# Two branches of an MLP cross SBUF in one transfer, and the fifth pair of sets is computed earlier

## The chip, the cores and the metric

The kernel runs on one core of a Trainium2 chip. The metric is the device time of one execution in microseconds (us). The kernel is written in Python; a scheduler places its instructions on the engines and sets every semaphore, and each engine then runs its own queue in order. The order of a queue follows the program's order in the main, but the scheduler may bring an instruction forward that it expects to be ready before an earlier one.

## The reference, cut to what matters

The model is an encoder trunk of two layers on 256 tokens of 1024 channels. Each layer has a mixer (pooling, attention, gates) and an MLP. Only the MLP is touched by the change:

```python
def _conv_ffn(xn, w_up, conv_w, conv_b, w_down):
    a, gval = jnp.split(xn @ w_up, 2, axis=-1)
    a = lax.conv_general_dilated(a, conv_w[:, None, :], ..., feature_group_count=D_FF) + conv_b
    return (jax.nn.gelu(a) * gval) @ w_down
```

`w_up` is 1024 x 5632 and `w_down` 2816 x 1024, all float32. The convolution has width 3 along the tokens, one filter per channel. The two halves of `xn @ w_up` are called the branches a and g here. 2816 channels are 22 chunks of 128.

## The kernel before

**Products.** Each float32 matrix is split into a high and a low part, and a product is made of three matmuls: high by high, high by low, low by high. For weights, `Weights` does this piece by piece: SP loads 1 MB of a weight matrix into one of three `raw` buffers (L120), ScalarE rounds half of it to the high part `wh` (L180), VectorE subtracts to get the low part `wl` (L181). So one load gives two pieces. Five pieces may be alive at once, and a piece is asked for three pieces ahead of its use. The next load is issued on SP when the buffer of the load three before is free, that is when the `wl` of both its pieces are done.

**Stages of the MLP.** `ORDER` (L39) writes out the order by hand. An entry `a`n or `g`n is a set: the a or g branch of the chunks 4n to 4n+3, made by `by_rows` (L599) from four pieces, 12 matmuls of 512 columns for each piece. `r5` is the last set: chunks 20 and 21 of both branches together. An entry `d`n is part n of the down projection, for chunks 4n to 4n+3, `residual_mm` (L528), again 12 matmuls for each chunk and one chunk a piece. Chunks 18 to 21 are held back and multiplied at the end, in segments, so that the residual sum and the norm of the next sub-layer can begin early. After each piece the function `unit()` (L1203) is called; so an entry of `ORDER` is four units, and the MLP has 64.

**From rows to channels.** A set comes out of `by_rows` with tokens on partitions, but the convolution and the down projection want channels there. `turn_up` (L1124) has VectorE transpose blocks of 32 x 32 (L1139, one instruction for each half t of the tokens) into a tile called `up_at`, and then `cross` (L611) has SP issue 16 DMAs that move the 32-partition blocks across partitions within SBUF. `cross` is a generator: each `unit()` takes it one step on, which is four DMAs (L616). Every set crosses by itself: a DMA moves 32 partitions x 256 floats, that is 32 KB in runs of 1 KB. The rows of all sets take turns in two buffers in the tile of tag `at2`. The g sets arrive in two buffers in the tile of tag `xn` (`up_xn` in the profile), the a sets and `r5` in tiles of the tags `gates` and `v0` (`up_turned`).

**Chunks.** `CHUNKS` (L40) says after which unit the chunk f is worked on by `up(f)` (L1150): ScalarE copies the crossed a chunk (L1155) and applies the middle tap and bias (L1157), VectorE adds the other taps (L1158, L1161), four more steps make the gelu (L1168, L1169, L1172, L1173), VectorE multiplies by the crossed g chunk (L1177), and L1180 and L1181 split the result in two parts for the down projection.

**Ends of the layers.** In the first layer, four pieces of the next layer's weights are split into the tags `m2`, `ybig` and `at2` while the down projection ends. Then L429 adds the sums to the residual, `Norm` (L417) squares and scales, and TensorE turns the result (L465).

Of the kernel before, what the change touches and what calls it, by code (L numbers as in the profile page):

```python
# [10 lines left out]
F32 = mybir.dt.float32  # L11
# [5 lines left out]
P = 128  # L17
# [10 lines left out]
NF = DFF // P  # L28
# [7 lines left out]

WARM = (5, 1, 2, 1)
PAIRS = (2, 4, 0, 1, 3, 5)
ORDER = "a0 g0 a1 g1 a2 g2 d0 a3 g3 d1 a4 g4 r5 d2 d3 d4"  # L39
CHUNKS = (13, 15, 17, 19, 21, 23, 25, 27, 29, 31, 33, 35, 41, 43, 45, 47, 53, 54, 56, 57, 58, 60)  # L40
VISITS = ((0, 1, 12, 14), (2, 3, 15, 16), (9, 10, 22, 23), (10, 11, 23, 24))
HALVES = (slice(0, 512), slice(512, D))
SEGMENTS = (HALVES, (slice(0, 512), slice(512, 768), slice(768, D)))
# [164 lines left out]
def encoder(ctx, tc, x, w_in, w_pool, pool_scale, w_a, w_b, w_o, norm1, norm2, w_up, conv_w,  # L208
# [4 lines left out]
    big = ctx.enter_context(tc.tile_pool(name="big", bufs=1))  # L213
# [15 lines left out]
    def rows(w, r0, n=2, c0=0, width=1024, tag=None, pieces=2):  # L229

        src = w[r0 : r0 + n * P, c0 : c0 + width].rearrange("(k p) c -> p k c", p=P)
        h = n // pieces
        return W.add(
            src, (n, width), [((lambda t, j=j: t[:, j * h : (j + 1) * h, :]), (h, width)) for j in range(pieces)],
            tag,
        )

    for l in range(DEPTH):
        for g in range(NG):
            c0 = C_V + g * 512  # L240
            slots = (("m2", 0, 2), ("m2", 1, 2), ("ybig",), ("at2",)) if g == 0 else ()
            for j in range(2):
                tag = "k1" if l == 0 and g == 1 and j == 0 else None
# [30 lines left out]
        slots = (("v1",), ("ybig",), ("at2",))  # L274
        for kind, n in ORDER.split():
            n = int(n)
            for j in range(2):
# [14 lines left out]
                else:  # L292
                    p = rows(w_up[l], j * 512, 4, (kind == "g") * DFF + 4 * n * P, 512)
# [7 lines left out]
    def gain(src):  # L301
        g = sm.tile([P, 2 * D], F32, tag="gain", bufs=1, name="gain")[:, 0:D]
        nc.sync.dma_start(out=g, in_=src.partition_broadcast(P))
        return g
# [281 lines left out]
    def v_tile():  # L586
        return acc.tile([P, 512], F32, tag="acc", name="v_ps")

    def v_sum(ps, x2, t, n, piece, of=4):

        _, (wh, wl) = piece
        passes = [(0, wh, 0), (0, wl, 0), (1, wh, 0), (0, wh, 1), (0, wl, 1), (1, wh, 1)]
        for m, (part, w, j) in enumerate(passes):
            nc.tensor.matmul(  # L594
                ps, x2[:, 2 * n + j, part, t, :], w[:, j, :], start=(n + m == 0),
                stop=(n == of - 1 and m == 5),
            )

    def by_rows(x2, of, visit=None):  # L599

        ps = [mmp.tile([P, 512], F32, tag="mm", name="rows_ps") for _ in range(2)]
        for n in range(of):
            piece = W.get()
            for t in range(2):
                v_sum(ps[t], x2, t, n, piece, of)
            W.free(piece[0])
            if visit:
                visit()
        return ps

    def cross(out, in_):  # L611

        for i in range(4):
            for j in range(4):
                a, b = slice(32 * i, 32 * i + 32), slice(32 * j, 32 * j + 32)
                nc.sync.dma_start(out=out[b, i], in_=in_[a, j])  # L616
            yield
# [174 lines left out]
    for l in range(DEPTH):  # L792
# [25 lines left out]
        else:  # L818
            for g in range(NG):
                held = begun[0] if g == 0 else [W.get() for _ in range(4)]  # L820
                for t in range(2):
                    if g + t == 0:
                        ps = begun[1]
                    else:
                        ps = v_tile()
# [15 lines left out]
        for gi in range(3, -1, -1):  # L841
# [8 lines left out]
            cur, n = u, S + 2 * PAD  # L850
            sh = 1
            while sh < w:
# [3 lines left out]
                    out=nxt[:, :, 0:n], in0=cur[:, :, 0:n], in1=cur[:, :, sh : sh + n]  # L856
# [7 lines left out]
            if hw > 1:  # L864
                e = edge[:, gi, hw : w - 1].unsqueeze(1).to_broadcast([P, 2, hw - 1])
                r = slice(o + S - hw + 1, o + S)
# [3 lines left out]
                out=pd, in0=cur[:, :, o : o + S], scalar=1.0 / w, in1=u[:, :, PAD : PAD + S],  # L870
# [34 lines left out]
        at2 = big.tile([P, HPG, 2, 2, P], F32R, tag="at2", name="at2")  # L905
        probs, ptiles, split, crossing = {}, {}, {}, []
# [90 lines left out]
        for m, c in enumerate(PAIRS):  # L997
# [4 lines left out]
            for n in range(4):  # L1002
# [5 lines left out]
                if hd < HPG:  # L1008
# [3 lines left out]
                        out=lo[:, hd], in0=src, scalar=scale, in1=hi[:, hd].bitcast(F32),  # L1012
# [3 lines left out]
                        out=lo[:, hd], in0=rest, scalar=scale, in1=lo[:, hd].bitcast(F32),  # L1016
                        op0=ALU.mult, op1=ALU.add,
                    )
                else:
# [3 lines left out]
                        out=o, in0=src, scalar=scale, in1=o, op0=ALU.mult, op1=ALU.add  # L1023
# [4 lines left out]
        for n, cc in enumerate(HALVES):  # L1028
            ps = by_rows(x2, 4, step)
# [30 lines left out]
        def keep_merged(c0, t, m):  # L1060
# [9 lines left out]
        g2 = gain(norm2[l])  # L1070
        nc.vector.transpose(
            out=way[:, 0].rearrange("p j t c r -> p (t c) j r"),
# [37 lines left out]
        g1 = gain(norm1[l + 1] if l + 1 < DEPTH else norm_f)  # L1110
# [8 lines left out]
        acts = {}  # L1119


        turned, ways = {}, []

        def turn_up(key, ps, tag):  # L1124

            if not ways:
                for own in ("at2", "xn"):
                    t = big.tile([P, 2, 4, 2, 4, 32], F32, tag=own, name="up_" + own)
                    ways.append([t[:, 0], t[:, 1]])
                ways.append([])  # L1130
            rows = ways[0].pop(0)
            ways[0].append(rows)
            if tag is None:
                out = ways[1].pop(0)
                ways[1].append(out)
            else:
                out = big.tile([P, 4, 2, 4, 32], F32, tag=tag, name="up_turned")
            for t in range(2):
                nc.vector.transpose(  # L1139
                    out=rows[:, :, t].rearrange("p j c r -> p c j r"),  # L1140
                    in_=ps[t].rearrange("p (c j r) -> p c j r", c=4, j=4),
                )
            ways[2].append(cross(out, rows))
            turned[key] = out.rearrange("p i t c r -> p c t i r")

        def blocks_in_order(a):

# [53 lines left out]
        count, chunk = 0, 0  # L1201

        def unit():  # L1203
            nonlocal count, chunk
            count += 1
            if ways and ways[2] and next(ways[2][0], "end") == "end":
                ways[2].pop(0)
                if ways[2]:
                    next(ways[2][0])
            while chunk < NF and CHUNKS[chunk] < count:  # L1210
                up(chunk)
                chunk += 1

        for kind, n in ORDER.split():
            if kind == "d":
                for _ in range(4):
                    next(down)
                    unit()
                continue
            if (kind, n) == ("a", "0"):  # L1220
                held, ps = entry
                ps = [ps, v_tile()]
                for k in range(4):
                    v_sum(ps[1], x2, 1, k, held[k])
                    unit()
                for i, _ in held:
                    W.free(i)
            else:
                ps = by_rows(x2, 4, unit)
            n = int(n)  # L1230
            turn_up((kind, n), ps, None if kind == "g" else ("gates", "v0")[n % 2])
        assert chunk == NF
        if l + 1 < DEPTH:
            x2 = two_parts("x", "x2")
            late["norm"] = Norm(to_channels(x2, mmp, g1))
# [33 lines left out]
```

## Time and profile before

| what | value |
|---|---|
| median of 3 runs | 878.66 us |
| lowest and highest of them | 875.95 and 880.52 us |
| the profiled execution | 878.63 us |
| its span, first to last instruction | 876.9 us |
| mean granted TensorE clock | 0.994 |
| VectorE busy | 653.6 us (75%) |
| ScalarE busy | 481.6 us (55%) |

The profiled execution lies 0.03 us from the median, and 1.73 us of it lie outside the span. Times in the rows below are microseconds from the start of the span. PE is TensorE's matmul, PEld its weight load, DVE is VectorE, ACT is ScalarE, SP is the engine whose queue issues the loads and the crossings. L12 is line 12 of the kernel. Where a row of the timeline has a count, several instructions are merged in it. The time in square brackets at the end of a row is the engine's idle time before it, with what ended it.

### The profile page before, as it was taken

To read this page: it belongs to the slowest core of one execution; us is meant where nothing else is said; L and a number is where in the kernel's file an instruction comes from. 1 tells how busy PE (TensorE), PEld (TensorE's weight loads), DVE (VectorE), ACT (ScalarE), POOL (GpSimd) and SP (SyncE) were. 2 spreads that over 40 slices of the span, in tenths; PEclk is the share of its full clock that TensorE was granted. 3 is DMA by queue.
4 is the path that set the end of the run, shared out by engine and by line. 5 is a ranking of instruction groups with operands and counts; after the bars stand their busy time and mean duration, and the time that the engine had idled before them with its cause. 6 is when DMAs were issued, how large, how long until landed. Compare 5 with 4: busy or idle time off the path is not lost.

```text
span 876.9 us, 11882 instructions
## 1 busy us (share of the span) xinstructions
PE 858.1 (98%) x4234; PEld 725.0 (83%) x4234; DVE 653.6 (75%) x1016; ACT 481.6 (55%) x777; POOL 21.2 (2%) x53
## 2 busy tenths in 40 slices
PE   9999999999999999999899999999999999999996
PEld 7888988888888887878788899888888888877885
DVE  6998786756866887688855968775567777876885
ACT  7755554543645656646635555454444456655573
POOL 2020000000000000000000000000000000000001
PEclk9999999999999999999999999999999999999998
DMA  9676546665737667666826455547557266676661
GB/s 333 211 221 222 202 129 211 191 224 185 265 117 232 200 221 255 216 196 211 313 101 219 165 194 191 178 158 243 202 195 272 96 220 197 225 237 213 222 224 48
DMA packets 114623, 178.76 MB, mean 204 GB/s; under 512 B 10542, under 2 KB 61950, under 8 KB 114564
## 3 DMA queue, kind: packets, MB, share of 16 engines
q1 hardware_dynamic: 114052, 176.67, 60.1%
q0 software_dynamic: 496, 1.33, 0.6%
q8 instruction: 33, 0.54, 0.2%
q14 instruction: 26, 0.21, 0.1%
q10 hardware_dynamic: 16, 0.00, 0.0%
HBM read 160.12 MB, written 1.07 MB: 184 GB/s over the span
## 4 chain that ended last, share of the span: by engine, by line
PE 85%; DVE 6%; DMA 5%; ACT 1%; SPq 1%; issue 1%; POOL 0%; POOLq 0%; DVEq 0%; ACTq 0%
PE rows_ps L594 37%; PE proj_ps L497 13%; PE proj_ps L499 7%; PE v_ps L594 6%; PE res_ps L524 4%; PE res_ps L525 4%; PE res_ps L526 4%; DVE wl L181 3%; PE v_ps L784 2%; DMA raw<-in_w_up_dram 2%; PE v_ps L697 1%; DMA up_turned<-up_at 1%; SPq L616 1%; DMA up_xn<-up_at 1%; PE o_ps L975 1%
## 5 line engine op out<-in xcount | busy, mean ns | idle before, releaser
L181 DVE TENSOR_TENSOR wl<-raw,wh 128x1024 fp32r<-128x1024 f32 x274 | 330.0, 1218 | 130.1 <-ACT wh L180 127.2
L180 ACT CAST wh<-raw 128x1024 fp32r<-128x1024 f32 x274 | 281.9, 1048 | 186.3 <-PE rows_ps L594 81.1
L594 PE MATMUL rows_ps<-wh,x 128*128 128x512 f32 x896 | 280.4, 390 | 0.0
L594 PEld LDWEIGHTS rows_ps<-wh,x 128*128 128x128 f32 x896 | 168.1, 188 | 34.6
L594 PE MATMUL rows_ps<-wl,x 128*128 128x512 f32 x448 | 175.1, 391 | 6.1 <-DVE wl L181 5.9
L497 PE MATMUL proj_ps<-x,wh 128*128 128x512 f32 x512 | 128.6, 393 | 0.0
L497 PEld LDWEIGHTS proj_ps<-x,wh 128*128 128x128 f32 x512 | 92.1, 189 | 16.5
L594 PEld LDWEIGHTS rows_ps<-wl,x 128*128 128x128 f32 x448 | 84.1, 188 | 25.7 <-DVE wl L181 8.7
L499 PEld LDWEIGHTS proj_ps<-x,wl 128*128 128x128 f32 x512 | 69.9, 190 | 5.1
L499 PE MATMUL proj_ps<-x,wl 128*128 128x256 f32 x512 | 71.5, 282 | 0.0
L525 PE MATMUL res_ps<-wl,actq 128*128 128x512 f32 (+1 forms) x184 | 70.3, 382 | 0.0
L526 PE MATMUL res_ps<-wh,actk 128*128 128x512 f32 (+1 forms) x184 | 69.9, 383 | 0.0
L524 PE MATMUL res_ps<-wh,actq 128*128 128x512 f32 (+1 forms) x184 | 63.4, 383 | 0.0
L1139 DVE STREAM_TRANSPOSE up_at<-rows_ps 128x512 f32<-128x512 f32 x40 | 28.2, 710 | 28.6 <-PE rows_ps L594 23.1
L524 PEld LDWEIGHTS res_ps<-wh,actq 128*128 128x128 f32 x184 | 35.1, 191 | 6.6
L525 PEld LDWEIGHTS res_ps<-wl,actq 128*128 128x128 f32 x184 | 35.0, 190 | 6.7
L526 PEld LDWEIGHTS res_ps<-wh,actk 128*128 128x128 f32 x184 | 35.0, 190 | 6.6
L594 PE MATMUL rows_ps<-wh,po 128*128 128x512 f32 x128 | 40.0, 389 | 0.0
L1180 ACT ACTIVATE actq<-g 128x256 fp32r<-128x256 f32 x44 | 17.8, 412 | 37.6 <-DVE g L1177 37.5
L1157 ACT ACTIVATE y<-a,prm 128x256 f32<-128x256 f32 x44 | 24.8, 595 | 8.2 <-DVE y L1173 8.2
L594 PEld LDWEIGHTS rows_ps<-wh,po 128*128 128x128 f32 x128 | 24.0, 188 | 5.0
L1168 ACT ACTIVATE y<-y 128x256 f32<-128x256 f32 x44 | 17.9, 408 | 17.4 <-DVE y L1161 17.4
(204 smaller groups left out, 1102.2 us busy)
## 6 DMA issues: line engine op xcount, KB each, us to landing
raw<-in_w_in_dram SPq DMA_DIRECT2D x58, 1024.0 KB, 6.0
raw<-in_w_up_dram SPq DMA_DIRECT2D x40, 1024.0 KB, 5.4
raw<-in_w_down_dram SPq DMA_DIRECT2D x22, 1024.0 KB, 5.1
raw<-in_w_a_dram SPq DMA_DIRECT2D x8, 1024.0 KB, 4.8
raw<-in_w_o_dram SPq DMA_DIRECT2D x8, 1024.0 KB
up_turned<-up_at SPq DMA_DIRECT2D x192, 32.0 KB, 4.0
up_xn<-up_at SPq DMA_DIRECT2D x160, 32.0 KB, 3.0
pt<-rows SPq DMA_DIRECT2D x64, 64.0 KB, 4.4
```

What stands on the lines that cost most here:

```text
L180: lambda: nc.scalar.copy(out=h, in_=src),
L181: lambda: nc.vector.tensor_sub(out=l, in0=src, in1=h.bitcast(F32)),
L497: nc.tensor.matmul(ps, wh(k), x2[:, k], start=(k == 0), stop=False)
L499: nc.tensor.matmul(ps[:, 1], wl(k), x2[:, k, 0], start=False, stop=(k == nk - 1))
L524: nc.tensor.matmul(ps, ah, wh, start=first, stop=False)
L525: nc.tensor.matmul(ps, ah, wl, start=False, stop=False)
L526: nc.tensor.matmul(ps, al, wh, start=False, stop=last)
L594: nc.tensor.matmul(ps, x2[:, 2 * n + j, part, t, :], w[:, j, :], start=(n + m == 0), stop=(n == of - 1 and m == 5),)
L1139: nc.vector.transpose(out=rows[:, :, t].rearrange("p j c r -> p c j r"), in_=ps[t].rearrange("p (c j r) -> p c j r", c=4, j=4),)
L1157: nc.scalar.activation(y, a, AF.Identity, bias=b, scale=w1)
L1168: nc.scalar.activation(y2, y, AF.Square, scale=float(np.sqrt(0.044715)))
L1180: nc.scalar.mul(out=ah, in_=g, mul=0.5)
```

## The change

The a and g branches of the same four chunks now share a pair of tiles: the rows of a and g lie beside each other, and after the g set one `cross` moves both, 64 KB in runs of 2 KB a DMA. The pairs take turns in two pairs of buffers, (`at2`, `xn`) and (`ybig`, `v1`). `r5`, which has both branches in one set, uses one half of its pair. `unit()` no longer starts the next crossing in the same unit in which one ends. In `ORDER`, `a4 g4` stand ahead of `d1`, and `CHUNKS` is even: one chunk every two units, after the units 13 to 35 and 41 to 59.

```diff
-ORDER = "a0 g0 a1 g1 a2 g2 d0 a3 g3 d1 a4 g4 r5 d2 d3 d4"
-CHUNKS = (13, 15, 17, 19, 21, 23, 25, 27, 29, 31, 33, 35, 41, 43, 45, 47, 53, 54, 56, 57, 58, 60)
+ORDER = "a0 g0 a1 g1 a2 g2 d0 a3 g3 a4 g4 d1 r5 d2 d3 d4"
+CHUNKS = (*range(13, 36, 2), *range(41, 60, 2))
...
-        turned, ways = {}, []
-
-        def turn_up(key, ps, tag):
-
-            if not ways:
-                for own in ("at2", "xn"):
-                    t = big.tile([P, 2, 4, 2, 4, 32], F32, tag=own, name="up_" + own)
-                    ways.append([t[:, 0], t[:, 1]])
-                ways.append([])
-            rows = ways[0].pop(0)
-            ways[0].append(rows)
-            if tag is None:
-                out = ways[1].pop(0)
-                ways[1].append(out)
-            else:
-                out = big.tile([P, 4, 2, 4, 32], F32, tag=tag, name="up_turned")
+        turned, pair, crossing = {}, [], []
+
+        def turn_up(kind, n, ps):
+
+            if kind != "g":
+                pair[:] = (
+                    big.tile([P, 4, 2, 2, 4, 32], F32, tag=tags[n % 2], name=name)
+                    for tags, name in ((("at2", "ybig"), "up_rows"), (("xn", "v1"), "up_turned"))
+                )
+            rows, out = (a[:, :, int(kind == "g")] for a in pair)
             for t in range(2):
                 nc.vector.transpose(
                     out=rows[:, :, t].rearrange("p j c r -> p c j r"),
                     in_=ps[t].rearrange("p (c j r) -> p c j r", c=4, j=4),
                 )
-            ways[2].append(cross(out, rows))
-            turned[key] = out.rearrange("p i t c r -> p c t i r")
+            turned[kind, n] = out.rearrange("p i t c r -> p c t i r")
+            if kind == "g":
+                crossing.append(cross(pair[1], pair[0]))
+            if kind == "r":
+                crossing.append(cross(out, rows))
...
-            if ways and ways[2] and next(ways[2][0], "end") == "end":
-                ways[2].pop(0)
-                if ways[2]:
-                    next(ways[2][0])
+            if crossing and next(crossing[0], "end") == "end":
+                crossing.pop(0)
...
-            turn_up((kind, n), ps, None if kind == "g" else ("gates", "v0")[n % 2])
-        assert chunk == NF
+            turn_up(kind, n, ps)
+        assert chunk == NF and not crossing
```

## The prediction

> **What bounds the kernel now.** I read the page's engine table first, then TensorE's waits, then the chain, because only these together tell how much of TensorE's time is work.
>
> ```profile
> span 876.9 us, 11882 instructions
> PE 858.1 (98%) x4234; PEld 725.0 (83%) x4234; DVE 653.6 (75%) x1016; ACT 481.6 (55%) x777; POOL 21.2 (2%) x53
> ```
> ```profile
> PE rows_ps L594 <- DVE wl L181: 5.9, 4, 1.5
> PE xt_ps L465 <- DVE xn L456: 2.7, 1, 2.7
> ```
> ```profile
> 263.59 54.40 PE rows_ps L594 x240
> ```
>
> The first line is the page's, then the waits of TensorE (us in total, times, longest), then a piece of the chain. TensorE is busy for 98%, and in the first 240 matmuls of an MLP's sets one starts every 54.40/240 = 0.227 us, back to back. The five waits listed, 5.9 + 2.7 = 8.6 us, are the idle time in which this change could find something: the program is TensorE's, and no faster crossing can shorten the matmuls. The Trainium skill says in Perfetto Trace Analysis, Identifying the Most-Contended Engine, that matmul busy time is a bad measure of the distance to the roofline and that the busy share of the weight loads is a good one; by its 83% some 17% of the span would be free, and the step of the matmuls speaks against that here.
>
> So the question is where the four waits for `wl` come from. They lie in the two MLPs, two in each, at the same places: the first piece of g3 and the first piece of g4.
>
> ```profile
> 339.13 0.39 PE L594 MATMUL rows_ps<-wl,x 128*128 128x512 f32 x1
> 339.36 0.84 PE L594 MATMUL rows_ps<-wh,x 128*128 128x512 f32 x3
> 341.66 0.50 PE L594 MATMUL rows_ps<-wl,x 128*128 128x512 f32 x1 [1.46 <-DVE wl L181]
> ...
> 386.50 0.84 PE L594 MATMUL rows_ps<-wh,x 128*128 128x512 f32 x3
> 387.45 0.50 PE L594 MATMUL rows_ps<-wl,x 128*128 128x512 f32 x1
> ```
> ```profile
> 335.16 1.99 ACT L180 CAST wh<-raw 128x1024 fp32r<-128x1024 f32 x2
> ```
> ```profile
> 321.03 1.18 DVE L181 TENSOR_TENSOR wl<-raw,wh 128x1024 fp32r<-128x1024 f32 x1
> ...
> 338.43 0.72 DVE L1139 STREAM_TRANSPOSE up_at<-rows_ps 128x512 f32<-128x512 f32 x1 [3.81 <-PE rows_ps L594]
> ...
> 339.79 0.72 DVE L1139 STREAM_TRANSPOSE up_at<-rows_ps 128x512 f32<-128x512 f32 x1
> 340.43 2.32 DVE L181 TENSOR_TENSOR wl<-raw,wh 128x1024 fp32r<-128x1024 f32 x2
> ```
>
> The timelines of TensorE, ScalarE and VectorE around 340 us. TensorE's third matmul of the row at 339.36 starts at 339.36 + 2 x 0.227 = 339.81, the next only at 341.66, so 341.66 - 339.81 - 0.227 = 1.62 us are lost. The `wh` of this piece began at 335.16, yet its `wl` runs at 340.43: in VectorE's queue it stands behind the two transposes of a3, and VectorE idles 3.81 us at the first of them until a3's sums are done. The order of the program has that `wl` ahead (it is asked for three pieces early), so the scheduler has moved the transposes forward, which it does when it expects the weights late. Are they late? SP's timeline tells.
>
> ```profile
> 322.69 0.53 SPq L120 DMA_DIRECT2D raw<-in_w_up_dram  x1
> ...
> 325.77 2.73 SPq L616 DMA_DIRECT2D up_xn<-up_at  x4
> 328.62 0.52 SPq L120 DMA_DIRECT2D raw<-in_w_up_dram  x1
> 329.18 5.48 SPq L616 DMA_DIRECT2D up_xn<-up_at  x8
> 334.76 0.53 SPq L120 DMA_DIRECT2D raw<-in_w_up_dram  x1
> 335.33 2.41 SPq L616 DMA_DIRECT2D up_xn<-up_at  x4
> 337.84 5.31 SPq L120 DMA_DIRECT2D raw<-in_w_down_dram  x2
> ```
> ```profile
> raw<-in_w_up_dram SPq DMA_DIRECT2D x40, 1024.0 KB, 5.4
> ```
> ```profile
> L616 SPq DMA_DIRECT2D up_turned<-up_at x192: 507/588/1735, 264.5 to 846.9; - x192
> L616 SPq DMA_DIRECT2D up_xn<-up_at x160: 507/588/894, 276.1 to 835.4; - x160
> ```
>
> SP has no idle time between 325.77 and 337.84 but for gaps of 0.1 us. The load at 328.62 carries g3's first two pieces; its buffer came free at 321.03 + 1.18 = 322.2 us, with the second `wl` of the load three before. It stood 6.4 us in SP's queue behind the crossings of g2, which by the program belong to d0's four units (from 318.0 us, where the chain's row ends, to 328.9) and are still being issued at 337. A load costs 5.44 us of TensorE (two pieces of 12 matmuls, 24 x 0.227); in that time SP must issue it and eight crossings, and from 322.69 to 328.62 to 334.76 that takes 5.93 and 6.14 us. **SP's issue rate, and through it the lateness of the weights, is what the waits hang on.** Past 337 the crossings pause and SP catches up.
>
> **The change part by part.** *Crossings.* A layer issues 11 sets x 16 = 176 DMAs now and 5 pairs x 16 + 16 for r5 = 96 afterwards; over both layers 352 (192 + 160 in the rows) become 192. At a median of 0.588 us, 160 fewer issues take 94 us off SP. The 64 KB form has its own rows in this trace, in the attention:
>
> ```profile
> L616 SPq DMA_DIRECT2D pt<-rows x64: 507/588/1628, 121.9 to 605.9; - x64
> DMA to landing us min/median/max: 1.9/4.4/5.3
> ```
>
> The issue is as dear as that of 32 KB (0.588 us), and the landing takes 4.4 us. So a pair's crossing keeps SP for four units as a single set's does, and then SP is free for four or more units, where now the crossings of a, g, a, g follow each other without a pause from unit 5 to unit 28. I take the lag of SP as gone between pairs: the load of g3 would be issued when its buffer is free, up to 6.4 us sooner. On TensorE this saves nothing by itself; what it saves is the waits: 1.62 us at g3, the same at g4, and at the first piece of r5 387.45 - 386.50 - 3 x 0.227 = 0.27 us, together 3.51 us a layer and 7.0 us in all. The bounds: nothing (the order on VectorE stays), and 7.0 us.
>
> *Two buffers in turn.* In the second layer the wait at g4 has another cause, which the change removes directly.
>
> ```profile
> 804.58 0.72 DVE L1139 STREAM_TRANSPOSE up_at<-rows_ps 128x512 f32<-128x512 f32 x1 [5.53 <-DMA up_xn<-up_at]
> ```
>
> The transpose of a4 waits 5.53 us for the crossing of an earlier set to have read its rows. With a whole pair of sets between two uses of a buffer, that crossing has 12 units, 12 x 2.72 = 33 us, and the wait is gone. This is within the 7.0 us.
>
> *Unchanged work.* 44 transposes, 44 copies (L1155), 44 multiplications (L1177) stay, in other strides but of the same size; I cost this at nothing, within the spread that L1177 shows now, 0.05 us either way each, off TensorE's path.
>
> ```profile
> L1177 DVE TENSOR_TENSOR g<-y,up_xn x40: 379/418/426, 293.5 to 845.6; 128x256 f32<-128x256 f32 x40
> ```
>  The tags `v1` and `ybig`, now taken, hold weights of a0 that are done after unit 4; the first pair that needs them is written at unit 12. Their next user is the next layer's weights, split from unit 62 on; r5's crossing, from unit 53, ends before.
>
> *A wait added.* The a branch used to arrive four units ahead of the g branch; now both arrive last. The copy L1155 of the first chunk comes after the sixth unit behind the g set: 6 x 2.72 = 16.3 us. The pair needs 1.4 us for the second transpose (339.79 - 338.43), 16 issues at 0.65 (the mean of 5.48/8 and 2.41/4), 10.3 us, two loads between them at 0.53, 1.1 us, and 4.4 us to land: 17.2 us. So the copy may wait about 0.9 us on ScalarE, and behind it stand the `wh` of the next pieces, and TensorE behind those. Their cover: `wh` at 335.16, TensorE's use at 339.81, less 1.0 for `wh` and 1.2 for `wl`, leaves 2.4 us. I take nothing for it; without that cover each pair would cost a stall of the size seen now.
>
> *`d1` moved behind a4 and g4, and the chunks.* d1 needs chunks 4 to 7, whose work is called at units 22 to 28, so it isn't held up; its two loads move in SP's queue past the four loads of a4 and g4 and the crossing of the fourth pair, and nobody waits for them sooner than for those. Chunks 16 to 21 come at units 50, 52, 54, 56, 58, 60, now 54, 55, 57, 58, 59, 61, and r5's crossing is no longer behind g4's. a3 to g4 are 16 units with transposes in a row; VectorE's load there is that of the run a0 to g2 and no stall is listed in that run:
>
> ```profile
> 263.60:328.70 65.10, 65.10 (x288) 53.88 (x288) 51.92 (x83) 37.48 (x63) 0.00 (x0) 1.00 0.68 219
> ```
>
> VectorE (third group) is busy 51.92 of 65.10 us. So the move is at nothing on TensorE.
>
> *The end of the first layer* is the fifth wait.
>
> ```profile
> 429.23 2.35 DVE L181 TENSOR_TENSOR m<-raw,m 128x1024 fp32r<-128x1024 f32 x2
> 431.50 1.22 DVE L181 TENSOR_TENSOR ybig<-raw,ybig 128x1024 fp32r<-128x1024 f32 x1
> 432.64 1.22 DVE L181 TENSOR_TENSOR at<-raw,at 128x1024 fp32r<-128x1024 f32 x1
> 433.78 2.21 DVE L429 TENSOR_TENSOR h<-res_ps,h 128x512 f32<-128x512 f32 x4
> ```
>
> The residual sums stand behind four splits of the next layer. TensorE too gets there sooner (3.5 us), so this wait shrinks only if VectorE gains more than TensorE; the last chunk moves a unit, 2.72 us, and r5's crossing by some more. Bounds 0 and 2.7 us; I take 0, since TensorE's gain and VectorE's nearly cancel.
>
> **The sum:** 878.63 - 7.0 = **871.6 us**, against the profiled execution and, as this is its median, against the runs.
>
> **Rivals.** *The order stays* (A). The loads may be sooner and the scheduler still put the transposes of a3 and a4 ahead of `wl`. For it speaks g4:
>
> ```profile
> 360.20 0.52 SPq L120 DMA_DIRECT2D raw<-in_w_up_dram  x1
> ```
> ```profile
> 372.86 0.72 DVE L1139 STREAM_TRANSPOSE up_at<-rows_ps 128x512 f32<-128x512 f32 x1 [6.06 <-PE rows_ps L594]
> ```
>
> Its load went out 12.7 us before VectorE stopped at a4's transpose, more than twice its landing time, and the transpose still went first. Then SP's 94 us are slack: 878.6 us, or 875.1 with half of the waits gone. This is also the case in which the change doesn't do what it says. The Trainium skill's DMA: Bandwidth & Descriptors, Issuing engines are not separate DMA queues, says that the sequencer's time for initiating a DMA is usually small beside the DMA itself; by that rule this rival holds. For the loads the trace agrees (0.53 against 5.4 us), for eight crossings in a row it does not.
>
> *The end shrinks too* (B): 871.6 - 2.7 = 868.9 us, if r5's earlier crossing lets VectorE finish chunk 21 and the four splits 2.7 us sooner than TensorE's own gain.
>
> *The pair comes too late* (C), the other side. SP issues in order, and a load whose buffer isn't free holds the crossings behind it: the two issues at 337.84 take 5.31 us, of which 5.31 - 2 x 0.53 = 4.25 us are such a wait. It makes 17.2 us into 21.4, past 16.3 + 2.4 = 18.7, from which on ScalarE's waiting copy reaches TensorE. At the 1.62 us of a present stall and ten pairs that is 16.2 us, with the old stalls gone 871.6 + 16.2 = 887.8 us; at half the pairs 879.7. Against it: the crossings of g2 were 8 us late and the scheduler simply placed their chunks' work later, with no wait of ScalarE for a crossing in its list.
>
> **How the numbers follow.** My forecast 0.44, A 0.26, B 0.10, C 0.20. About 0.5% (4.4 us) is what a measurement of this kernel tells from no change. Faster by more (under 874.2): the forecast and B, 0.44 + 0.10 = 0.54. Within: A and C's weak end, at half the pairs, 0.26 + 0.03 = 0.29. Slower (over 883.0): the rest of C, 0.17. The range goes from 868.5, just under B, to 884, which takes in A and C's weak end and leaves out about 0.15 of C above; the forecast's own range is 870 to 874.
>
> **What would show it.** In the changed profile 192 issues of L616 in the MLP at about 0.59 us; loads issued within 1 us of their buffer's release around g3; `wl` of the first pieces of g3, g4 and r5 ahead of the transposes, and TensorE's wait for `wl` at under 2 us in total. A is right if that wait stays near 5.9 us; C if ScalarE's or VectorE's waits name a crossing (L1155 behind `up_turned`) and TensorE's rise. I am wrong altogether if TensorE's step of 0.227 us changes while 64 KB crossings run, since then SBUF traffic and not order is what counts.

## The result, and the profile after

| kernel | median of 4 runs | lowest to highest |
|---|---|---|
| before | 879.46 us | 875.95 to 880.52 us |
| after | 870.83 us | 870.71 to 870.96 us |

The ratio of the means (as all ratios below) is 0.9909, with a 95% interval of 0.9880 to 0.9938: 0.9% faster. The forecast was 871.6 us. The profiled execution took 870.80 us, with a span of 869.0 us. One of the four executions of e5 below took 1072.78 us at a granted clock of 0.751 and is left out there. The engine table of the kernel after, then TensorE's waits:

```profile
PE 855.7 (98%) x4234; PEld 723.9 (83%) x4234; DVE 652.4 (75%) x1016; ACT 482.7 (56%) x777; POOL 21.8 (3%) x53
```
```profile
PE xt_ps L465 <- DVE xn L456: 1.9, 1, 1.9
PE rows_ps L594 <- DVE wl L181: 1.2, 2, 0.6
```

The matmuls are as many as before. The listed wait for `wl` went from 5.9 us in four places to 1.2 us in two, and the wait at the end of the first layer from 2.7 to 1.9 us. The step of the matmuls is unchanged, 54.40/240 = 0.227 us in the chain, and the crossings are the 192 foreseen, at the same 0.588 us of SP each (the first three figures of the second row: shortest, median and longest in ns):

```profile
263.26 54.40 PE rows_ps L594 x240
```
```profile
L616 SPq DMA_DIRECT2D up_turned<-up_rows x192: 507/588/1318, 275.0 to 835.9; - x192
```

Now the place that the prediction began with, the change from a3 to g3 near 339 us. SP's timeline of the kernel after, then VectorE's:

```profile
320.96 0.53 SPq L120 DMA_DIRECT2D raw<-in_w_up_dram  x1
321.53 6.25 SPq L616 DMA_DIRECT2D up_turned<-up_rows  x8
...
329.62 2.41 SPq L616 DMA_DIRECT2D up_turned<-up_rows  x4
...
358.33 2.41 SPq L616 DMA_DIRECT2D up_turned<-up_rows  x4
```
```profile
318.34 2.32 DVE L181 TENSOR_TENSOR wl<-raw,wh 128x1024 fp32r<-128x1024 f32 x2
...
333.79 1.23 DVE L181 TENSOR_TENSOR wl<-raw,wh 128x1024 fp32r<-128x1024 f32 x1
...
338.10 0.72 DVE L1133 STREAM_TRANSPOSE up_rows<-rows_ps 128x512 f32<-128x512 f32 x1 [0.37 <-PE rows_ps L594]
```

The `wl` pair at 318.34 ends at 320.66 and frees a buffer; SP issues the load into it at 320.96, 0.30 us later, where it was 6.4 us before. After the third pair's crossings SP issues no crossing from 332.0 to 358.3 us. And on VectorE the `wl` of g3's first piece (333.79) now stands ahead of a3's transposes (338.10); TensorE passes from a3 to g3 without a wait.

What is left lies one set further, in the first two pieces behind g3, which in the new order is a4. (An expectation below that calls a wait left over in the changed kernel g4 means this place.) VectorE, ScalarE and TensorE of the kernel after:

```profile
348.98 0.72 DVE L1133 STREAM_TRANSPOSE up_rows<-rows_ps 128x512 f32<-128x512 f32 x1 [3.76 <-PE rows_ps L594]
349.62 1.19 DVE L181 TENSOR_TENSOR wl<-raw,wh 128x1024 fp32r<-128x1024 f32 x1
```
```profile
351.18 0.60 ACT L1154 ACTIVATE y<-a,prm 128x256 f32<-128x256 f32 x1 [3.59 <-DVE y L1170]
...
352.17 1.04 ACT L180 CAST wh<-raw 128x1024 fp32r<-128x1024 f32 x1
```
```profile
349.92 0.84 PE L594 MATMUL rows_ps<-wh,x 128*128 128x512 f32 x3
350.86 0.50 PE L594 MATMUL rows_ps<-wl,x 128*128 128x512 f32 x1
...
353.04 0.84 PE L594 MATMUL rows_ps<-wh,x 128*128 128x512 f32 x3
354.46 0.50 PE L594 MATMUL rows_ps<-wl,x 128*128 128x512 f32 x1 [0.58 <-DVE wl L181]
```

It is the old picture at a smaller price. VectorE idles 3.76 us at g3's transpose with `wl` queued behind it, and behind that a gelu step (L1170), on which ScalarE stands 3.59 us with the next `wh` behind it. TensorE loses 350.86 - 349.92 - 3 x 0.227 = 0.26 us at the first piece and 354.46 - 353.04 - 3 x 0.227 = 0.74 us at the second, 1.00 us a layer.

The end of the first layer, TensorE of the kernel before, then after: the last residual matmul ahead of the norm, the norm's first transpose, and a later matmul of the same work.

```profile
434.72 0.28 PE L526 MATMUL res_ps<-wh,actk 128*128 128x256 f32 x1
437.65 0.66 PE L465 MATMUL xt_ps<-ident,xn 128*128 128x128 f32 x2 [2.65 <-DVE xn L456]
...
440.45 0.28 PE L524 MATMUL res_ps<-wh,actq 128*128 128x256 f32 x1
```
```profile
431.63 0.28 PE L526 MATMUL res_ps<-wh,actk 128*128 128x256 f32 x1
433.84 0.41 PE L465 MATMUL xt_ps<-ident,xn 128*128 128x128 f32 x2 [1.93 <-DVE xn L456]
...
435.38 0.28 PE L524 MATMUL res_ps<-wh,actq 128*128 128x256 f32 x1
```

The same stretch takes 440.45 - 434.72 = 5.73 us before and 435.38 - 431.63 = 3.75 us after. Of the 1.98 us saved, 2.65 - 1.93 = 0.72 are a shorter wait. The other 1.26 are the same matmuls at a slower clock before: in the windows of the two kernels the sixth figure behind the length is the granted clock.

```profile
436.00:440.00 4.00, 2.35 (x11) 2.38 (x12) 2.18 (x6) 1.60 (x6) 1.56 (x4) 0.63 0.70 261
```
```profile
433.00:436.00 3.00, 2.16 (x19) 2.19 (x20) 2.64 (x7) 0.79 (x3) 0.98 (x3) 1.00 0.60 227
```

**Where the time came from.** From rows of the two traces: at the start of the row of 240 matmuls the kernel after is 263.59 - 263.26 = 0.33 us ahead, before any of the change has run; at the last residual matmul 434.72 - 431.63 = 3.09 us, so 2.76 us come from the first MLP; 1.98 us come from the layer's end; and of the spans' 876.9 - 869.0 = 7.9 us the remaining 7.9 - 0.33 - 2.76 - 1.98 = 2.8 us come after that, from the second MLP: its own row of 240 starts 695.28 - 690.24 = 5.04 us ahead, as the first layer left it.

### The profile page after: what moved, and what is told of

Same layout as the page of the kernel before. It is cut to its first block, busy times and chain, and to the rows that moved or that the text cites. A ratio compares the mean times of both kernels' runs of the same rounds, so it can differ in the third digit from the quotient of the medians.

```text
span 869.0 us, 11682 instructions
## 1 busy us (share of the span) xinstructions
PE 855.7 (98%) x4234; PEld 723.9 (83%) x4234; DVE 652.4 (75%) x1016; ACT 482.7 (56%) x777; POOL 21.8 (3%) x53
## 4 chain that ended last, share of the span: by engine, by line
PE 93%; DVE 4%; ACT 1%; DMA 1%; issue 1%; POOL 0%; POOLq 0%; DVEq 0%; ACTq 0%
PE rows_ps L594 42%; PE proj_ps L497 14%; PE proj_ps L499 7%; PE v_ps L594 6%; PE res_ps L524 5%; PE res_ps L525 5%; PE res_ps L526 5%; PE v_ps L784 3%; DVE wl L181 2%; PE v_ps L697 1%; PE o_ps L975 1%; PE s_ps L918 1%; PE o_ps L971 1%; PE s_ps L913 1%; PE xt_ps L465 1%; DMA raw<-in_w_in_dram 1%
## 5 line engine op out<-in xcount | busy, mean ns | idle before, releaser
L524 PE MATMUL res_ps<-wh,actq 128*128 128x512 f32 (+1 forms) x184 | 67.0, 380 | 0.0
L1133 DVE STREAM_TRANSPOSE up_rows<-rows_ps 128x512 f32<-128x512 f32 x40 | 27.9, 709 | 24.1 <-PE rows_ps L594 24.1
```

The lines of the kernel that those rows point to most:

```text
L524: nc.tensor.matmul(ps, ah, wh, start=first, stop=False)
L1133: nc.vector.transpose(out=rows[:, :, t].rearrange("p j c r -> p c j r"), in_=ps[t].rearrange("p (c j r) -> p c j r", c=4, j=4),)
```

## The experiments

The **first theory** is the prediction's chain of causes: SP's crossings make loads late, so the scheduler puts a set's transposes ahead of the next set's `wl` on VectorE, so TensorE waits; crossing in pairs relieves SP. The main rivals were that the new `ORDER` and `CHUNKS` do it alone, and that the order on VectorE is the cause whatever SP does. The first four runs made the last of these the **new theory**, and the other eight test it and what it leaves unexplained. Ratios are to runs of the kernel before on the same chip (medians 879.85 for the first four, 880.74 for e5, e8, e9 and e10, 880.46 for e6, e7, e11 and e12).

### Half of the change: pairs with the old order (e1)

```diff
# against the kernel after
-ORDER = "a0 g0 a1 g1 a2 g2 d0 a3 g3 a4 g4 d1 r5 d2 d3 d4"
-CHUNKS = (*range(13, 36, 2), *range(41, 60, 2))
+ORDER = "a0 g0 a1 g1 a2 g2 d0 a3 g3 d1 a4 g4 r5 d2 d3 d4"
+CHUNKS = (13, 15, 17, 19, 21, 23, 25, 27, 29, 31, 33, 35, 41, 43, 45, 47, 53, 54, 56, 57, 58, 60)
```

> The pairs cross together in 2 KB runs, with two buffers in turn, but the order and the chunks' units are those of before. Theory (SP's issue load makes the weights late, so the scheduler sets transposes ahead of the low parts): most of the gain is here, TensorE's wait for the low parts at the first pieces of g3 and g4 falls from 5.9 us to under 2 us in all, and the time is 872 to 874 us. Rival (the gain is the move of a4 g4 ahead of d1): that wait stays at 5 to 6 us and the time at 878 to 880 us.

Measured: 881.77 us, 1.0022 (1.0011 to 1.0033). Both numbers missed. The waits at g3 and g4 are gone, but 0.50 us have come behind g3, which is d1 in this order, and a longer wait at r5's first piece. VectorE, TensorE, and a window of this kernel:

```profile
383.69 0.72 DVE L1133 STREAM_TRANSPOSE up_rows<-rows_ps 128x512 f32<-128x512 f32 x1 [0.34 <-PE rows_ps L594]
...
385.63 1.22 DVE L181 TENSOR_TENSOR wl<-raw,wh 128x1024 fp32r<-128x1024 f32 x1
```
```profile
386.91 0.50 PE L594 MATMUL rows_ps<-wl,x 128*128 128x512 f32 x1 [2.81 <-DVE wl L181]
...
388.23 0.63 PE L594 MATMUL rows_ps<-wh,x 128*128 128x512 f32 x1
388.66 0.63 PE L594 MATMUL rows_ps<-wl,x 128*128 128x512 f32 x1
```
```profile
388.00:391.00 3.00, 3.00 (x9) 2.33 (x8) 3.00 (x5) 2.12 (x4) 0.00 (x0) 0.50 0.23 27
```

The `wl` of r5 stands behind g4's transposes, and behind the wait of 2.81 us the clock is granted at 0.50: matmuls start 388.66 - 388.23 = 0.43 us apart instead of 0.227. Pairs alone move the wait and make it dearer.

### The other half: the new order with single crossings (e2)

```diff
# against the kernel before
-ORDER = "a0 g0 a1 g1 a2 g2 d0 a3 g3 d1 a4 g4 r5 d2 d3 d4"
-CHUNKS = (13, 15, 17, 19, 21, 23, 25, 27, 29, 31, 33, 35, 41, 43, 45, 47, 53, 54, 56, 57, 58, 60)
+ORDER = "a0 g0 a1 g1 a2 g2 d0 a3 g3 a4 g4 d1 r5 d2 d3 d4"
+CHUNKS = (*range(13, 36, 2), *range(41, 60, 2))
```

> The order and the chunks' units are those of the change, but each set crosses by itself in 1 KB runs as before. Theory: SP issues 176 crossings a layer as before, so the wait for the low parts stays at 4 to 6 us and the time is 877 to 880 us. Rival (the move of a4 g4): the wait falls to under 2 us and the time is 871 to 874 us.

Measured: 874.45 us, 0.9934 (0.9922 to 0.9947), between the theories. g3's wait stays, g4's is gone, a smaller one comes at d2. TensorE at g3:

```profile
341.13 0.50 PE L594 MATMUL rows_ps<-wl,x 128*128 128x512 f32 x1 [1.46 <-DVE wl L181]
```

So g3's wait hangs on the crossings (gone in e1, here not), g4's goes with either half, and neither half alone gives the whole gain.

### The order on VectorE forced, nothing else (e3 and e4)

```diff
# e3 against the kernel before; e4 is the same against the kernel after
                     for make in part:
-                        make()
+                        self.lows[i] = make()
...
             for t in range(2):
-                nc.vector.transpose(
+                with ExitStack() as behind:
+                    if W.n_got in W.lows:
+                        behind.enter_context(tc.issue_after(W.lows[W.n_got].ins))
+                    nc.vector.transpose(
```

`lows[i]` is the `wl` of piece i; a set's transposes now queue behind the `wl` of the next piece, where that has been made.

> The kernel before with one thing added: a set's transposes are queued on VectorE behind the low part of the next piece that TensorE uses. SP's load is untouched. Theory's last link (the order on VectorE's queue is what TensorE waits on; the weights themselves have landed in time): the four waits of 1.5 us go, the time is 872 to 874 us. Rival (the weights really come too late): VectorE waits for the load instead, TensorE's wait stays near 5.9 us, the time is 878 to 880 us.

> The changed kernel with the same added order. Theory: what is left of TensorE's waits at g4 (0.27 + 0.75 us a layer) goes, so the time is 1 to 2 us under the changed kernel's 870.8, 869 to 870 us. Rival (these waits are of another kind): 870.8 us, no change.

Measured: e3 867.64 us, 0.9860 (0.9844 to 0.9877), better than expected; e4 868.27 us, 0.9869 (0.9853 to 0.9884), a little better too. The expectation for e3 counted the waits for `wl` alone: of the 876.9 - 865.6 = 11.3 us by which its span is shorter, 4.0 and 4.1 lie in the two MLPs, 2.65 at the end of the first layer and 0.56 ahead of the first MLP. In e3 SP issues the same crossings and is as late. VectorE, SP and the first of TensorE's waits in e3, the longest in total:

```profile
320.47 1.19 DVE L182 TENSOR_TENSOR wl<-raw,wh 128x1024 fp32r<-128x1024 f32 x1
...
336.89 2.35 DVE L182 TENSOR_TENSOR wl<-raw,wh 128x1024 fp32r<-128x1024 f32 x2
339.17 1.31 DVE L1143 STREAM_TRANSPOSE up_at<-rows_ps 128x512 f32<-128x512 f32 x2
```
```profile
328.38 0.52 SPq L121 DMA_DIRECT2D raw<-in_w_up_dram  x1
```
```profile
PE xt_ps L466 <- DVE xn L457: 1.3, 1, 1.3
```

The buffer is free at 320.47 + 1.19 = 321.66 and the load goes out at 328.38, 6.7 us later, much as in the kernel before; yet the longest wait that TensorE has left is the 1.3 us at the layer's end, and none for `wl` is listed. So a late load doesn't reach TensorE by itself here; the order on VectorE does. And e3, without any pair, is faster than the changed kernel: 0.9860 against 0.9909, intervals apart.

### The new order with the order on VectorE forced (e10)

The two edits of e2 and e3 together.

> The change's order and chunk units, each set crossing by itself as before, and transposes queued behind the next low part. New theory: 867 to 870 us, like the kernel before and the changed kernel with this order on VectorE (867.6 and 868.3). Rival (crossing together is worth something of its own): over 1 us slower than the changed kernel with this order, 869.5 us or more.

Measured: 867.44 us, 0.9862 (0.9842 to 0.9882), as the new theory expected. Against e4, 0.9869, which is the same with crossings in pairs: once the order on VectorE is right, crossing together is worth nothing that can be measured. e3, e10 and e4 are the fastest kernels of this study that do the whole computation; by their intervals they can't be told from each other.

### Pairs, old order, forced (e8)

The edits of e1 and e4 together.

> The pairs crossing together in the order of before (881.8 us without more), with a set's transposes queued on VectorE behind the next piece's low part. New theory (the order on VectorE's queue alone makes the waits, the form of the crossing has no part in it): the wait at r5 goes and the time is 867 to 870 us. Rival (with pairs the weights of r5 are really late, ScalarE waits 5 us for a load twice there): the wait stays, 874 to 880 us.

Measured: 874.11 us, 0.9938 (0.9914 to 0.9963). The time lies in the rival's range, but both causes named there missed: no wait for `wl` is left. What holds TensorE is `actq`, the result of the last chunks:

```profile
428.27 0.50 PE L525 MATMUL res_ps<-wh,actq 128*128 128x512 f32 x1 [2.00 <-ACT actq L1181]
```

With d1 ahead of a4 and g4, r5's crossing queues behind the whole of the fifth pair's. The last crossings on SP in e8, and in e4, which differs in the order alone:

```profile
409.58 5.30 SPq L617 DMA_DIRECT2D up_turned<-up_rows  x8
```
```profile
405.70 2.41 SPq L617 DMA_DIRECT2D up_turned<-up_rows  x4
```

They end at 414.88 in e8 and at 408.11 in e4, 6.8 us later. So crossing in pairs needs the fifth pair of sets earlier, which is what the change's new order does.

### Single crossings in the changed kernel (e6)

```diff
# against the kernel after
-            if kind == "g":
-                crossing.append(cross(pair[1], pair[0]))
-            if kind == "r":
-                crossing.append(cross(out, rows))
+            crossing.append(cross(out, rows))
...
                 crossing.pop(0)
+                if crossing:
+                    next(crossing[0])
```

> The changed kernel with its buffers, order and chunk units, but each set crosses by itself right after it, in 1 KB runs. If crossing together is what removes the wait at g3, it is back here, 1.5 us a layer, and the time is 873 to 876 us, as with the order alone (874.5). If the buffers in turn remove it: 870 to 872 us.

Measured: 876.81 us, 0.9963 (0.9952 to 0.9975), a little over the 873 to 876 expected. g3's wait is back, with the new buffers and the new order in place:

```profile
341.34 0.50 PE L594 MATMUL rows_ps<-wl,x 128*128 128x512 f32 x1 [1.47 <-DVE wl L181]
```

So it is crossing together that removes this wait, not the two buffers in turn.

### The same pairs in runs of 1 KB (e7)

```diff
# against the kernel after: cross_halves is cross with
+                for e in range(2):
+                    nc.sync.dma_start(out=out[b, i, e], in_=in_[a, j, e])
...
-                crossing.append(cross(pair[1], pair[0]))
+                crossing.append(cross_halves(pair[1], pair[0]))
```

> The changed kernel, but a pair crosses at the same moment in 1 KB runs: eight DMAs of 32 KB a unit instead of four of 64 KB, so SP issues 176 crossings a layer as before. First theory (SP's issue load sets the transposes ahead at g3): the wait at g3 is back and the pairs land later, 876 us or more. Rival (at g3 it matters that a and g arrive together and late, not what SP spends): no wait at g3, TensorE's wait for low parts stays near the changed kernel's 1.2 us, 870 to 873 us.

Measured: 907.82 us, 1.0321 (1.0276 to 1.0366). Eight DMAs a unit are more than SP can issue: at 10.38/16 = 0.65 us each they take 5.2 us of a unit's 2.72. SP, VectorE, then ScalarE:

```profile
330.04 0.53 SPq L120 DMA_DIRECT2D raw<-in_w_up_dram  x1
330.62 10.38 SPq L625 DMA_DIRECT2D up_turned<-up_rows  x16
341.10 0.53 SPq L120 DMA_DIRECT2D raw<-in_w_up_dram  x1
```
```profile
338.76 2.36 DVE L181 TENSOR_TENSOR wl<-raw,wh 128x1024 fp32r<-128x1024 f32 x2
...
341.38 1.31 DVE L1142 STREAM_TRANSPOSE up_rows<-rows_ps 128x512 f32<-128x512 f32 x2
```
```profile
347.52 1.99 ACT L180 CAST wh<-raw 128x1024 fp32r<-128x1024 f32 x2 [7.52 <-DMA raw<-in_w_up_dram]
```

The load at 330.04 carries g3's first two pieces. It goes out 5.6 us after its buffer was free (at 324.43, where the `wl` pair at 322.07 ends), yet their `wl` (338.76) stands ahead of a3's transposes (341.38), and TensorE has no wait at g3's first piece. In e6 the same load is 5.7 us late (free at 323.05, issued at 328.75) and the transposes stand ahead. So at g3 the rival's half holds, no wait when a and g cross together whatever SP spends, while its time missed; the first theory has the time and missed the wait.

What costs the time is another thing. The load at 341.10, for g3's third and fourth pieces, is 8.9 us late (free at 332.24), and now the late load itself reaches TensorE: ScalarE stands 7.52 us for it. The loads of the kernel before, late by 6.4 us, and of e3, by 6.7, didn't. This run issues 352 crossings, as e3 does; here they come bunched. The Trainium skill, in DMA: Bandwidth & Descriptors, Issuing engines are not separate DMA queues, calls the sequencer's time for starting a DMA usually small beside the DMA. For one crossing the trace agrees (0.65 us to issue, 2.8 us to land); for eight in a unit the sum decides, and this kernel takes 907.82 - 870.83 = 37 us more than with four.

### The crossings on GpSimd's queue (e5)

```diff
# against the kernel before, for the MLP's crossings
-            ways[2].append(cross(out, rows))
+            ways[2].append(cross(out, rows, nc.gpsimd))
```

> The kernel before, with the crossings of the MLP issued on GpSimd's queue instead of SP's: their number, size and buffers are those of before, but SP issues loads alone. First theory (SP's queue, full of crossings, is what sets the transposes ahead of the low parts): TensorE's wait for low parts falls under 2 us, 871 to 874 us. Rival (the order on VectorE turns on when crossings land and chunks can be worked on, not on SP's load): waits of the present size remain somewhere, 876 to 882 us.

Measured: 901.25 us (the median of three), 1.0238 (1.0202 to 1.0273); both ranges missed. SP's loads go out in time and g3's wait is gone, but now the crossings are late. The longest of ScalarE's waits in the first MLP, and ScalarE's timeline:

```profile
ACT a L1155 <- DMA up_xn<-up_at: 26.3, 3, 11.0
```
```profile
395.25 0.42 ACT L1155 COPY a<-up_turned 128x256 f32<-128x256 f32 x1 [11.03 <-DMA up_xn<-up_at]
395.57 1.04 ACT L180 CAST wh<-raw 128x1024 fp32r<-128x1024 f32 x1
```

This is rival C's mechanism: the copy L1155 waits 11.03 us for a crossing, and a `wh` stands behind it. GpSimd issues a crossing in a median of 0.498 us, so the rate isn't the reason; why its queue fell behind was not tried further.

### No crossing at all (e11)

```diff
# against the kernel before
-            rows = ways[0].pop(0)
-            ways[0].append(rows)
...
+            rows = out
...
-            ways[2].append(cross(out, rows))
```

> The kernel before with the MLP's crossings left out: the blocks are read where VectorE turned them, so the MLP's sums are taken over wrongly placed blocks. It bounds what any cheaper crossing can bring. New theory (crossings cost TensorE nothing by themselves, the order on VectorE makes its waits): not under the 867.5 us that the right order reaches with all crossings, 866 to 880 us depending on the order that comes out. First theory: all waits for low parts gone, 866 to 870 us.

Measured: 863.56 us, 0.9817 (0.9796 to 0.9839), under what both theories said. TensorE waits for nothing but the start of the program, 1.0 and 0.2 us in its first 8 us. All the MLP's crossings together cost 867.4 - 863.6, about 4 us, once the order on VectorE is right, and nearly none of it inside the MLPs: against e10 these take 0.02 and 0.33 us less, the stretch between them 1.4 us less, and the time behind the last matmul 2.5 us less.

### The fault multiplied (e12)

```diff
# against the kernel before: the next piece's low part queues behind each set's transposes
+                if self.turned is not None:
+                    queued.enter_context(self.tc.issue_after(self.turned.ins))
+                    self.turned = None
...
+            if key[0] + str(key[1]) != "a0":
+                W.turned = last
```

For this the look-ahead of the pieces is cut at the end of each set, too; no run has that cut alone.

> The suspected cause multiplied: the kernel before with the low part of the next piece queued on VectorE behind the transposes of every set but the first, where now this is so at g3 and g4. New theory: each of some ten places a layer costs TensorE 1.6 us, twenty in all 33 us, less the 7 us of today's: 900 to 912 us. Rival (the order alone costs little, today's waits come from late weights): under 885 us.

Measured: 909.08 us, 1.0335 (1.0309 to 1.0361), as expected. TensorE's waits, and two places of TensorE's timeline:

```profile
PE rows_ps L600 <- DVE wl L187: 22.8, 14, 3.0
PE res_ps L531 <- DVE wl L187: 6.1, 6, 1.0
```
```profile
276.70 0.50 PE L600 MATMUL rows_ps<-wl,x 128*128 128x512 f32 x1 [1.47 <-DVE wl L187]
...
290.15 0.50 PE L600 MATMUL rows_ps<-wl,x 128*128 128x512 f32 x1 [2.28 <-DVE wl L187]
```

Twenty places wait now, twelve of them for 1.46 or 1.47 us, as at 276.70, the size of the two old waits (1.46 and 1.49). The order makes the stall and its size in most places where it is put.

### Two of the next layer's splits held back (e9)

```diff
# against e3
+            if self.n_got < self.late.get(i, 0):
+                break
...
+    W.late = {n_first + 2: n_first + 1, n_first + 3: n_first + 1}
```

> The kernel before with transposes queued behind the next low part (867.6 us), and two of the four splits of the next layer's weights made after the residual sums at the end of the first layer. Theory: the wait at the end of the first layer comes from the splits that stand ahead of the residual sums on VectorE; it goes, with the slow matmuls behind it: 865 to 866.5 us. Rival (these splits are needed just then): the next layer's first sums wait for them, 867.5 us or more.

Measured: 869.39 us, 0.9883 (0.9860 to 0.9906), no gain over e3. TensorE at the end of the first layer:

```profile
431.99 0.41 PE L470 MATMUL xt_ps<-ident,xn 128*128 128x128 f32 x2 [1.13 <-DVE xn L461]
```

With fewer splits ahead of the residual sums the wait is still 1.13 us, where e3 lists 1.3 and the kernel before 2.7; e2, e6 and e10 list 1.1 too, with all four splits ahead and VectorE waiting for the last residual matmuls. So the last 1.1 us are the norm's own chain, and only what lies above that is VectorE being behind. The rival's time came out, but not its mechanism: the next layer's first sums wait 0.2 us.

## Why the prediction was right, and where its terms were off

The total came within 0.8 us of the forecast, but through two terms that were mis-sized in opposite directions; that it came so close is in part luck.

- **What bounds the kernel** held: TensorE's step didn't change, and what changed were its waits and, at one place, its clock.
- **SP's relief** held as a fact: the load of g3 goes out 0.30 us after its buffer's release. As the cause it isn't shown. "**SP's issue rate, and through it the lateness of the weights, is what the waits hang on**" said too much: the waits hang on the order on VectorE (e3, e12). At g3 this order is wrong with single crossings on SP (before, e2, e6) and right with pairs (after, e1) or with the crossings off SP (e5); but it is right in e7, too, where SP is as loaded and the load as late (5.6 us) as in e6 (5.7 us). So crossing in pairs can put it right without a load that is issued sooner. What the scheduler goes by is open; no run measured its estimates. g4's wait goes with either half (e1, e2).
- **The reading of g4** for rival A was off: its load went out 12.7 us before the transpose ran at 372.86, but VectorE had stopped there 6.06 us sooner, at 366.80, 6.6 us after the load.
- **The 7.0 us of stalls** are the mis-sized term. They came to 2.76 + 2.8 = 5.6 us. The three old waits did go, 3.51 us a layer, but the same fault turned up behind g3 for 1.00 us a layer: 3.51 - 1.00 = 2.51 of the 2.76 us measured in the first MLP; 0.25 us I can't place. The prediction took the old waits' places to be the only ones.
- **Two buffers in turn**: no transpose waits for a crossing in the kernel after, as foreseen. But this was no other cause of g4's wait in the second layer, which is 1.49 us in both layers and goes in e2 with the old buffers as well.
- **The move of `d1` at nothing** was wrong as a step: with the new `CHUNKS`, from which no run parts it, it brings 0.66% of the 0.91% by itself (e2). Pairs without it run at 1.0022 (e1), and even with the order forced at 0.9938 (e8), because r5's crossing then queues behind the fifth pair's.
- **The end of the first layer at nothing** is the second mis-sized term: 1.98 us of its bounds 0 and 2.7. The argument that TensorE's gain and VectorE's nearly cancel accounts for the listed wait, which shrank by 0.72 us; but the prediction had no term for the slow clock behind a wait, which was 1.26 us. Whether the clock drops isn't decided by the wait's length alone: at this same place e1 waits 3.31 us and its clock stays at 1.00. So that part of the gain can't be counted on.
- **Copies, multiplications and the transposes in new strides at nothing** held: their medians are 0.416, 0.422 and 0.716 us, where they were 0.416, 0.418 and 0.711, and TensorE waits for none of them.
- **Rival A** fell at g3 and held in small at the place behind g3. Of the Trainium skill's rule beside it, that starting a DMA costs little, e3 and e7 show the two sides: it holds for four issues a unit and not for eight.
- **Rival B** was right in part: the end shrank, by 0.72 us of wait and not 2.7, while the rest gave less than forecast.
- **Rival C** did not happen: in the kernel after no wait of ScalarE for an MLP crossing is listed. Its mechanism is real once crossings are late enough (e5); the changed kernel stays under that point.

## What to carry to other kernels

When an engine with time to spare holds up the busiest one, look in its in-order queue for an instruction that waits for the busy engine's current result and stands ahead of what that engine needs next; fixing that order directly (e3, e10: 1.4%) gave more than the change (0.9%), which set it right in some places and not in others. Try the two halves of a change apart, and each with the suspected fault removed: here one half alone was slower, and once the order was right, crossing together had no worth of its own that could be measured. A total that comes out as forecast says little about its terms until each has been read in the trace.

## What the runs showed of the hardware

- The granted clock can drop behind short waits, and the length of the wait alone doesn't decide it. Behind an idle time of 2.28 us (e12), 2.65 (before) and 2.81 us (e1, at r5) the clock falls to 0.50 for about 3 us, in which matmuls step at 0.43 us; behind 1.93 (after) and 2.07 us (e4) it stays at 1.00. But it also stays at 1.00 behind 2.35 us in e7 and behind 3.31 us in e1, at the end of the first layer, where the same two matmuls take 0.41 us that take 0.66 in the kernel before:

```profile
440.29 0.41 PE L465 MATMUL xt_ps<-ident,xn 128*128 128x128 f32 x2 [3.31 <-DVE xn L456]
```

- The Trainium skill, in TensorE: Matmul & The Clock Gate, What's actually happening, gives at least one idle window of about 3.4 us as the condition for the slow clock; these runs show the drop after less.
- A crossing of 64 KB costs SP the same median of 0.588 us as one of 32 KB: of these DMAs it is the number, not the bytes, that loads the issuing queue.
